# The FFN's down projection: seven-product 2x2 blocks in two sweeps, or the plain product into eight PSUM banks

## The chip, the cores and the metric

The kernel runs on one core of one Trainium2 chip. The metric is the device time of one execution in microseconds (us). The core has TensorE (PE, matrix products; PEld is its loading of the stationary operand), VectorE (DVE), ScalarE (ACT), GpSimd (POOL) and SyncE (SP, which issues most of the DMA transfers). The engines run side by side and wait for one another by semaphores.

## The reference, cut to what matters

One layer of a decoder trunk with 512 tokens, 1024 channels and a feed-forward network (FFN) of 2816 inner channels, all in float32. The change concerns the last product, `@ w_down`, of shape 512x2816 by 2816x1024.

```python
def conv_glu_ffn(h, w_up, conv_w, w_down):
    a, g = jnp.split(h @ w_up, 2, axis=-1)
    return (jax.nn.silu(causal_dwconv(a, conv_w)) * g) @ w_down
...
        h = rmsnorm(x, norm_ffn[l]) * (1 + sc2) + sh2
        x = x + g2 * conv_glu_ffn(h, ffn_w_up[l], ffn_conv_w[l], ffn_w_down[l])
    return rmsnorm(x, final_norm)
```

## The kernel before, in words

**Products in two parts.** Every float32 operand of a large product is split into a rounded part (`hi`, type float32r, a copy by ACT) and the rest (`lo`, a subtraction by DVE). A product is then three matmuls into one PSUM bank: hi by hi, hi by lo, lo by hi. A matmul here takes a stationary operand of 128x128 and a moving one of 128x512 or 128x256.

**Order.** The code names buffers and operations; a scheduler puts the instructions of each engine in one fixed order, by their dependences and by priorities (`tc.high_priority`, `urgent`). An engine works its list off in that order; an instruction that waits holds up all behind it on its engine. SP's list of transfers works the same way.

**Stages.** The branches of the mixer, their gates and the merge come first, then the output projection with the residual, then the FFN's up projection, then its down projection with the closing norm. In the trace the up projection runs from about 820 us on and the down projection from about 1071 us to the end.

**Up projection (lines 1001 to 1203).** For each block `m` of 128 inner channels it forms 2x2 block products, seven in place of eight, in `product` (matmuls of 128x256 at lines 1053 to 1055). DVE's adds at lines 1185, 1194, 1195 and 1201 take the products out of PSUM; the conv is at lines 689 to 691, the gate at line 1202, and the result goes into the tile `f`, 22 blocks of 128x512. Per block, lines 1016, 1017 and 1046 split the weights, and POOL's lines 1034 to 1037 form their sums. The last product of all is `last()` (line 1203), twelve matmuls named `sd<-mg_hi,h_hi` and the like; its bank is free for it once line 1195 has read it. Tile names in a row are those of the memory's first user: `mg_hi`, `mg_lo`, `h_hi` and `h_lo` hold parts of `f` in the down stage.

**Down projection (lines 1205 to 1389).** The 22 blocks of `f` are taken in 11 pairs. The even and odd block of a pair, the two token halves and the two column halves make 2x2 blocks. `sweep1` forms four of the seven products for all pairs, `sweep2` the other three on top of copies of those. Per pair, `sweep1` has

- three sums of `f` blocks on POOL and one on DVE (lines 1266 to 1271), and their splits, line 1249 on ACT and line 1250 on DVE,
- two sums of weight blocks on POOL and one on DVE (lines 1273 to 1275), and the splits of the four weight blocks, line 1236 on ACT and line 1237 on DVE,
- 4 products x 2 token blocks x 3 matmuls of 128x512 (line 1257).

`sweep2` reads the weights again (lines 1242 to 1246), forms sums at lines 1310 to 1312, splits in the same way and has 3 x 2 x 3 matmuls per pair. After the last three pairs, `finish` and `residual` (lines 1333 and 986) multiply by `g2`, add the residual `x_end`, take the norm and store the rows, a token block after another.

**Buffers.** Raw weights land in four buffers (`wraw`), in `sweep2` in `h_hi` and `h_lo` as well. Split weights lie in two rings of three pairs, `whi`/`wlo` and `shi`/`slo`. Split `f` lies in six slots, two in the tiles `h_hi`/`h_lo` and four in `mg_hi`/`mg_lo`; those four are in use by the up projection until `last()` is done.

```python
    def down(ps, i, a, ai, w, wi, first=False, last=False):
        t = slice(i * 128, (i + 1) * 128)
        ops = [(0, 0), (0, 1), (1, 0)]
        for n, (x, y) in enumerate(ops):
            PE.matmul(ps, a[x][:, ai, t], w[y][:, wi], start=first and n == 0, stop=last and n == 2, skip_group_check=True)
```

Of the kernel before, what the change touches and what calls it, by code (L numbers as in the profile page):

```python
# [59 lines left out]
def hybrid_block(ctx, tc, ins, out, consts, dbg=None, stop=99):  # L60
# [196 lines left out]
    def ada_first(c0, n):  # L257
        """Chunks c0..c0+n of the first two parts of the modulation, not yet summed over partitions."""
# [88 lines left out]
    def rel_pos(name, shape, aps, pos0, pool, keep=None):  # L347
        """Positions less the first one, in float32: exact however large they are, as long as the differences are exact."""
# [11 lines left out]
    def bias_operands():  # L360
# [16 lines left out]
        # scaled by a power of two to magnitudes under 2^15, and split into two parts of 11 bits  # L377
# [905 lines left out]
    for j in range(n_pairs):  # L1283
        sweep1(j)
# [136 lines left out]
```

## Time and profile before

| what | value |
|---|---|
| time, median of 3 runs (lowest, highest) | 1248.59 us (1246.18, 1259.89) |
| span of the profiled execution, first to last instruction | 1246.3 us |
| time around that span | none is listed; the median lies 2.3 us above it |
| busy share of the span: PE, DVE, POOL, ACT | 86%, 76%, 42%, 40% |
| mean granted clock of PE | 0.950 |

The page of the profile is of one execution. A busy share is a mean over stages of different kinds; the stretch of a stage, its waits and the order of its instructions say what bounds it. The clock is a fraction of full speed: 1.00 is 2.4 GHz, 0.5 is 1.2 GHz, and a value between is a mixture over time.

### The profile page before, as it was taken

Reading aid. Unit: us, or ns where it says so; the run is one execution under the profiler, and the core shown is the slowest. Engines: PE = TensorE matmul, PEld = TensorE weight load, DVE = VectorE, ACT = ScalarE, POOL = GpSimd, SP = SyncE. Lnnn points to the kernel's source line nnn. Section 1 sums busy time; section 2 is a strip of 40 time slices with the busy share of each in tenths; the row PEclk is TensorE's granted clock in tenths of the full one; section 3 lists DMA queues with packets and bytes.
Section 4 is the critical chain, followed back from the end, with each engine's and each line's share of the span. In section 5 each row is a group of like instructions: output and inputs, shape, how many; then the busy total and the mean of one; then the engine's idle time right before and its main releaser. Section 6 shows DMA issues by size and latency. Waiting matters only on the chain.

```text
span 1246.3 us, 18485 instructions
## 1 busy us (share of the span) xinstructions
PE 1076.5 (86%) x6896; PEld 871.0 (70%) x6896; DVE 945.3 (76%) x1538; ACT 495.6 (40%) x890; POOL 522.9 (42%) x372
## 2 busy tenths in 40 slices
PE   4798999799999799888989999989888887679665
PEld 3676678577667768665666788889888886557444
DVE  6778777532789378976655444899898898999997
ACT  4243422242434244223434333665445454444442
POOL 3232223322222415554541000156566565776762
PEclk9789999899989899988999999989999999899898
DMA  9632123412348933698653535312323232244611
GB/s 313 174 86 71 39 60 102 95 35 66 107 150 253 303 96 86 193 235 218 179 134 98 145 101 166 115 51 85 92 79 101 73 99 85 76 170 168 218 53 68
DMA packets 194247, 156.97 MB, mean 126 GB/s; under 512 B 18499, under 2 KB 167389, under 8 KB 194157
## 3 DMA queue, kind: packets, MB, share of 16 engines
q1 hardware_dynamic: 165773, 131.22, 36.1%
q10 hardware_dynamic: 23056, 14.53, 3.9%
q0 software_dynamic: 5328, 10.03, 3.6%
q8 instruction: 54, 0.88, 0.3%
q14 instruction: 36, 0.29, 0.1%
HBM read 137.13 MB, written 18.63 MB: 125 GB/s over the span
## 4 chain that ended last, share of the span: by engine, by line
PE 39%; DVE 37%; issue 10%; DMA 6%; ACT 4%; POOL 2%; SPq 0%; ACTq 0%; DVEq 0%; POOLq 0%
PE mm L177 6%; PE mm L179 6%; PE mm L178 6%; DVE wlo L1237 3%; DMA xraw<-in_ada_w 3%; DVE acc L217 2%; DVE mg_lo L1250 2%; DVE h_lo L1046 2%; DVE slo L1237 2%; DVE slo L1017 2%; DVE acc L271 2%; PE sd L801 2%; DVE sub L571 1%; PE sd L727 1%; PE sd L800 1%
## 5 line engine op out<-in xcount | busy, mean ns | idle before, releaser
L165 POOL TENSOR_TENSOR wlo<-wraw,whi 128x1024 fp32r<-128x1024 f32 (+1 forms) x70 | 154.2, 2204 | 279.8 <-ACT whi L163 225.7
L178 PE MATMUL mm<-h_lo,whi 128*128 128x512 f32 (+2 forms) x496 | 201.8, 407 | 1.2 <-DVE h_lo L1082 1.2
L177 PE MATMUL mm<-h_hi,whi 128*128 128x512 f32 (+2 forms) x496 | 202.1, 408 | 0.7 <-DVE o_cv L702 0.7
L179 PE MATMUL mm<-h_hi,wlo 128*128 128x512 f32 (+2 forms) x496 | 201.3, 406 | 0.0
L163 ACT ACTIVATE whi<-wraw 128x1024 fp32r<-128x1024 f32 (+1 forms) x86 | 80.1, 934 | 222.2 <-PE mm L178 91.8
L178 PEld LDWEIGHTS mm<-h_lo,whi 128*128 128x128 f32 (+1 forms) x496 | 95.7, 193 | 23.5 <-issue 2.5
L177 PEld LDWEIGHTS mm<-h_hi,whi 128*128 128x128 f32 (+1 forms) x496 | 95.4, 193 | 22.4 <-issue 3.2
L179 PEld LDWEIGHTS mm<-h_hi,wlo 128*128 128x128 f32 (+1 forms) x496 | 95.6, 193 | 21.4 <-issue 1.5
L1053 PE MATMUL sd<-mg_hi,shi 128*128 128x256 f32 x240 | 70.1, 292 | 18.0 <-DVE p L1185 17.8
L1034 POOL TENSOR_TENSOR fS<-wraw 128x512 f32<-128x512 f32 x20 | 29.8, 1490 | 129.2 <-DMA wraw<-in_ffn_w_up 125.6
L217 DVE SCALAR_TENSOR_TENSOR acc<-xraw,ccol,acc 128x512 f32<-128x512 f32 x56 | 60.5, 1080 | 23.0 <-DMA xraw<-in_ada_w 22.5
L1055 PE MATMUL sd<-mg_hi,slo 128*128 128x256 f32 x240 | 68.1, 284 | 0.0
L1054 PE MATMUL sd<-mg_lo,shi 128*128 128x256 f32 x240 | 68.0, 283 | 0.0
L1017 DVE TENSOR_TENSOR slo<-fS,shi 128x1024 fp32r<-128x1024 f32 x40 | 60.5, 1512 | 0.5 <-ACT shi L1016 0.4
L1053 PEld LDWEIGHTS sd<-mg_hi,shi 128*128 128x128 f32 x240 | 45.9, 191 | 21.1 <-DVE p L1185 21.1
L1017 DVE TENSOR_TENSOR wlo<-wraw,whi 128x1024 fp32r<-128x1024 f32 x27 | 34.0, 1260 | 20.2 <-ACT whi L1016 20.1
L1053 PE MATMUL mm<-h_hi,whi 128*128 128x256 f32 x160 | 46.1, 288 | 3.0 <-ACT p L1066 3.0
L721 DVE TENSOR_SCALAR mk<-posq,thr 128x512 f16<-128x512 f32 (+3 forms) x128 | 44.7, 421 | 4.1 <-PE sd L727 4.1
L1016 ACT ACTIVATE shi<-fS 128x1024 fp32r<-128x1024 f32 x40 | 42.1, 1052 | 10.7 <-PE sd L1054 10.5
L1054 PEld LDWEIGHTS sd<-mg_lo,shi 128*128 128x128 f32 x240 | 46.0, 192 | 0.0
L1055 PEld LDWEIGHTS sd<-mg_hi,slo 128*128 128x128 f32 x240 | 45.9, 191 | 0.0
L1054 PE MATMUL mm<-h_lo,whi 128*128 128x256 f32 x160 | 45.6, 285 | 0.0
(565 smaller groups left out, 3120.6 us busy)
## 6 DMA issues: line engine op xcount, KB each, us to landing
wraw<-in_w_in SPq DMA_DIRECT2D x61, 512.0 KB, 4.1
xraw<-in_ada_w SPq DMA_DIRECT2D x96, 256.0 KB, 4.2
wraw<-in_ffn_w_up SPq DMA_DIRECT2D x44, 512.0 KB, 3.8
wraw<-in_ffn_w_down SPq DMA_DIRECT2D x17, 512.0 KB, 3.5
wraw<-in_w_branch SPq DMA_DIRECT2D x24, 256.0 KB, 3.6
bias_d<-stage ACTq DMA_DIRECT2D x10, 512.0 KB, 5.8
wraw<-in_w_o SPq DMA_DIRECT2D x8, 512.0 KB, 3.8
h_hi<-in_ffn_w_down SPq DMA_DIRECT2D x8, 512.0 KB, 4.5
```

Source lines behind the costliest of these rows:

```text
L163: ACT.activation(hi, raw, AF.Copy)
L165: lo_engine[0].tensor_tensor(lo, raw, hi, op=ALU.subtract)
L177: PE.matmul(ps, hi[:, k, :], ahi[:, k0 + k, :], start=start and k == 0, stop=False)
L178: PE.matmul(ps, hi[:, k, :], alo[:, k0 + k, :], start=False, stop=False)
L179: PE.matmul(ps, lo[:, k, :], ahi[:, k0 + k, :], start=False, stop=stop and k == kt - 1)
L217: DVE.scalar_tensor_tensor(acc, raw, ck, acc, op0=ALU.mult, op1=ALU.add)
L721: DVE.tensor_scalar(m_[:, :n], posq[:, b * 128:], thr[:, b, gg:gg + 1], None, op0=ALU.is_ge)
L1017: DVE.tensor_tensor(lo, src, hi, op=ALU.subtract)
L1053: PE.matmul(ps, at(w[0], k), b[0][:, k], start=first and k == 0, stop=False, skip_group_check=True)
L1054: PE.matmul(ps, at(w[0], k), b[1][:, k], start=False, stop=False, skip_group_check=True)
L1055: PE.matmul(ps, at(w[1], k), b[0][:, k], start=False, stop=k == 3, skip_group_check=True)
L1237: DVE.tensor_tensor(lo[:, d], src, hi[:, d], op=ALU.subtract)
```

## The change

The down projection is formed directly. Each of the 22 blocks of `ffn_w_down` (128x1024) is loaded once and split once, by `pair` (line 1016 on ACT, line 1017 on DVE); each pair of `f` blocks is split once, as 128x1024 (line 1219 on ACT, line 1220 on DVE). All eight PSUM banks, four token blocks by two column halves, are filled at once: 22 x 8 x 3 matmuls of 128x512 (lines 1238 to 1240). The sums of blocks, the second reading of the weights and the copies between the sweeps are gone. The last two pairs are kept back and run bank by bank, so that the closing norm of a token block can run while the next is multiplied. The up projection's code is the same. Comments and docstrings are gone from the file too. The core of the diff:

```diff
-    sd, mm = [sd_bank() for _ in range(5)], [mm_bank() for _ in range(3)]
-    p1b, p5b, p6b, p7b = sd[:2], [sd[2], mm[0]], mm[1:], sd[3:]
+    n_pairs, n_tail = 11, 2
+    banks = [mm_bank() for _ in range(3)] + [sd_bank() for _ in range(5)]
...
-    def sweep1(j):
-        ra, rb = rows_of(2 * j, 0, D), rows_of(2 * j + 1, 512, 512)
-        b11, b12 = ra[:, 0:512], ra[:, 512:D]
-        a11, a21, a12, a22 = (f[:, 2 * j + x, t] for x, t in ((0, t1), (0, t2), (1, t1), (1, t2)))
-        u = next_slot()
-        s1, s2, s3 = sn("p1"), sn("p5"), sn("p6")
-        t12 = T("fS", [128, 2, 512], bufs=2, pool=fs.pool)
-        POOL.tensor_tensor(s1, a21, a22, op=ALU.add)
-        DVE.tensor_tensor(s3, a11, a21, op=ALU.subtract)
-        POOL.tensor_tensor(s2, s1, a11, op=ALU.subtract)
-        for i, src in enumerate((a11, s1, s2, s3)):
-            split_a(u, i, src.unsqueeze(1))
-        POOL.tensor_tensor(a21, a12, s2, op=ALU.subtract)
-        with tc.high_priority(offset=4000):
-            POOL.tensor_tensor(t12[:, 0], b12, b11, op=ALU.subtract)
-            POOL.tensor_tensor(t12[:, 1], rb, t12[:, 0], op=ALU.subtract)
-            DVE.tensor_tensor(rb, rb, b12, op=ALU.subtract)
-        w12 = w_tile(2, (b11, t12[:, 0]))
-        w34 = w_tile(2, (t12[:, 1], rb))
...
-    def sweep2(j):
...
-        split_a(u, 0, ff_flat[:, j * 1024 + N2:(j + 1) * 1024].rearrange("p (i t) -> p i t", t=N2))
-        t4 = T("fS", [128, 2, 512], bufs=2, pool=fs.pool)
-        with tc.high_priority(offset=4000):
-            DVE.tensor_tensor(t4[:, 0], rb[:, 0:512], rb[:, 512:D], op=ALU.subtract)
-            POOL.tensor_tensor(t4[:, 1], ra[:, 512:D], ra[:, 0:512], op=ALU.subtract)
-            POOL.tensor_tensor(t4[:, 0], t4[:, 0], t4[:, 1], op=ALU.add)
-        w56 = w_tile(2, (rb,))
-        w7 = w_tile(1, (t4[:, 0],))
...
+    def split_pair(j):
+
+        u = slots[j if j < 2 else 2 + (j - 2) % 4]
+        src = ff_flat[:, j * 1024:(j + 1) * 1024].rearrange("p (a t) -> p a t", t=u[0].shape[2])
+        ACT.activation(u[0], src, AF.Copy)
+        DVE.tensor_tensor(u[1], src, u[0], op=ALU.subtract)
+        return u
...
+    def w_down(m):
+        raw = load_raw([128, D], [((lambda r: r), dram("ffn_w_down", m * 128 * D, [[D, 128], [1, D]]))])
+        ring = n_ring[0] // 3 % 2
+        n_ring[0] += 1
+        return pair([128, D], raw, ws if ring else None)
+
+    def down(tb, hf, u, m, w, first=False, last=False):
+        ps, c = banks[tb * 2 + hf], slice(hf * 512, hf * 512 + 512)
+        hi, lo = (f_cols(x, m, tb) for x in u)
+        PE.matmul(ps, hi, w[0][:, c], start=first, stop=False)
+        PE.matmul(ps, hi, w[1][:, c], start=False, stop=False)
+        PE.matmul(ps, lo, w[0][:, c], start=False, stop=last)
...
     for j in range(n_pairs):
-        s = sweep2(j)
...
+        u = split_pair(j)
+        for m in range(2):
+            w = w_down(2 * j + m)
+            if j >= n_pairs - n_tail:
+                tail.append((u, m, w))
+                continue
+            for tb in range(4):
+                for hf in range(2):
+                    down(tb, hf, u, m, w, first=j == 0 and m == 0)
+        if j == 1:
             SP.dma_start(g2, g2_d)
...
+        if 2 <= j < 6:
+            SP.dma_start(x_end[j - 2], x1_d[j - 2])
+        if j == 6:
+            SP.dma_start(fnorm, dram("final_norm", 0, [[0, 128], [1, D]]))
             ACT.activation(sqrt_table, one, AF.Sqrt)
...
+    for tb in range(4):
+        for hf in (1, 0):
+            for t_ in tail:
+                down(tb, hf, *t_, last=t_ is tail[-1])
+            residual(x_end[tb], hf, banks[tb * 2 + hf], g2, ss[:, tb])
+            if hf:
+                POOL.tensor_tensor(x_end[tb][:, c_hi], x_end[tb][:, c_hi], fnorm[:, c_hi], op=ALU.mult)
+        finish(tb)
```

The instructions of every engine stand in the same order in both programs up to the last blocks of the up projection. The first place is DVE there, between the read of block 20's bank (the first `L1195` row; `p` with a number is a block's copied product) and the read of block 21's bank (the second), behind which `last()` starts. Before, in `L1237`, `L1275` the down stage's work:

```order
L1195 TENSOR_TENSOR wk<-sd,p_9905 128x256
L1237 TENSOR_TENSOR wlo<-wraw,whi 128x512 x2
L1237 TENSOR_TENSOR slo<-fS,shi 128x512
L1275 TENSOR_TENSOR wraw<-wraw 128x512
L1237 TENSOR_TENSOR wlo<-fS,whi 128x512
L1202 TENSOR_TENSOR f<-f,wk 128x512
L1185 TENSOR_TENSOR p_9986<-sd,p_9810 128x256
L1237 TENSOR_TENSOR slo<-wraw,shi 128x512 x2
L1194 TENSOR_TENSOR wk<-sd,p_9986 128x256
L1275 TENSOR_TENSOR wraw<-wraw 128x512
L1237 TENSOR_TENSOR slo<-fS,shi 128x512
L1195 TENSOR_TENSOR wk<-sd,p_9985 128x256
```

The same place in the changed program, where the splits of whole weight blocks (`slo<-wraw`) are the down stage's work:

```order
L1195 TENSOR_TENSOR wk<-sd,p_9905 128x256
L1201 TENSOR_TENSOR wk<-sd,p_9552 128x256
L1017 TENSOR_TENSOR slo<-wraw,shi 128x1024
L1202 TENSOR_TENSOR f<-f,wk 128x512
L690 SCALAR_TENSOR_TENSOR f<-wk,fw,f 128x511
L1201 TENSOR_TENSOR wk<-sd,p_9681 128x256
L691 SCALAR_TENSOR_TENSOR f<-wk,fw,f 128x510
L1185 TENSOR_TENSOR p_9986<-sd,p_9810 128x256
L1017 TENSOR_TENSOR slo<-wraw,shi 128x1024
L1194 TENSOR_TENSOR wk<-sd,p_9986 128x256
L1202 TENSOR_TENSOR f<-f,wk 128x512
L1195 TENSOR_TENSOR wk<-sd,p_9985 128x256
```

Nine operations of the down stage have become two of twice the width, and five of the up stage's own (line 1201 twice, lines 690, 691 and 1202, of earlier blocks) have moved in.

The second place is DVE within the down stage: `mg_lo` rows split `f`, `wlo` and `slo` rows split weights, `fS` rows form sums of weights. Before, early in the second sweep:

```order
L1250 TENSOR_TENSOR mg_lo<-f,mg_hi 128x768
L1237 TENSOR_TENSOR slo<-h_hi,shi 128x1024
L1250 TENSOR_TENSOR mg_lo<-f,mg_hi 128x768
L1237 TENSOR_TENSOR slo<-fS,shi 128x512
L1310 TENSOR_TENSOR fS<-h_lo 128x512
L1237 TENSOR_TENSOR wlo<-h_hi,whi 128x1024
L1250 TENSOR_TENSOR mg_lo<-f,mg_hi 128x768
L1237 TENSOR_TENSOR wlo<-fS,whi 128x512
```

In the changed program, from behind `last()` on:

```order
L1220 TENSOR_TENSOR mg_lo<-f,mg_hi 128x1024 x4
L1017 TENSOR_TENSOR wlo<-wraw,whi 128x1024 x3
L1017 TENSOR_TENSOR slo<-wraw,shi 128x1024 x2
L1220 TENSOR_TENSOR mg_lo<-f,mg_hi 128x1024
L1017 TENSOR_TENSOR slo<-wraw,shi 128x1024
L1017 TENSOR_TENSOR wlo<-wraw,whi 128x1024
L1220 TENSOR_TENSOR mg_lo<-f,mg_hi 128x1024
```

All sums are gone from the list; from here on it holds 16 weight blocks and 9 pairs of `f`, and then the closing norm.

The third place is SP's list of transfers, which shows where loads other than weights stand. `f<-g_d` is the row `g2`, `f<-x_d` the residual rows; both land in parts of `f` and wait until those have been split. Before, around the turn from the first to the second sweep, where the weights come in blocks and half blocks and into `h_hi` too:

```order
L147 DMA wraw<-in_ffn_w_down 128x1024
L147 DMA wraw<-in_ffn_w_down 128x512
L147 DMA wraw<-in_ffn_w_down 128x1024
L1245 DMA h_hi<-in_ffn_w_down 128x1024
L147 DMA wraw<-in_ffn_w_down 128x512
L147 DMA wraw<-in_ffn_w_down 128x1024
```

In the changed program, the whole stage:

```order
L147 DMA wraw<-in_ffn_w_down 128x1024 x2
L1269 DMA f<-g_d 128x1024
L147 DMA wraw<-in_ffn_w_down 128x1024 x3
L1271 DMA f<-x_d 128x1024
L147 DMA wraw<-in_ffn_w_down 128x1024 x5
L1271 DMA f<-x_d 128x1024 x3
L147 DMA wraw<-in_ffn_w_down 128x1024
L1273 DMA f<-in_final_norm 128x1024
L147 DMA wraw<-in_ffn_w_down 128x1024 x11
L1255 DMA out_dram<-f 128x512 x8
```

Each block of the weights now appears once, 22 in all, and the other loads stand among the first eleven.

## Rows read from the trace of the kernel before

**Rows 1.** The page, part 1: busy time, share of the span, instructions.

```profile
PE 1076.5 (86%) x6896; PEld 871.0 (70%) x6896; DVE 945.3 (76%) x1538; ACT 495.6 (40%) x890; POOL 522.9 (42%) x372
```

**Rows 2.** Windows: stretch, length, busy per engine, PE's clock, DMA share, GB/s.

```profile
680.00:780.00 100.00, 100.00 (x447) 80.16 (x446) 46.45 (x62) 38.83 (x57) 7.67 (x8) 1.00 0.50 140
1028.95:1072.59 43.64, 30.70 (x231) 28.99 (x230) 38.45 (x46) 19.55 (x36) 28.82 (x22) 0.96 0.27 86
1072.59:1235.60 163.01, 122.82 (x470) 91.84 (x468) 159.18 (x185) 67.00 (x128) 104.71 (x75) 0.92 0.36 127
```

**Rows 3.** Waits of PE from 1072.5 to 1236 us: total, times, longest.

```profile
PE sd L1257 <- DVE mg_lo L1250: 18.3, 8, 4.9
PE sd L1257 <- DVE slo L1237: 9.5, 3, 7.2
PE mm L1257 <- DVE h_lo L1250: 4.7, 1, 4.7
PE sd L1257 <- DVE wlo L1237: 3.8, 4, 1.4
PE sd L1257 <- ACT f L1292: 2.1, 2, 1.5
PE mm L1257 <- DVE mg_lo L1250: 1.8, 2, 1.2
```

**Rows 4.** Timeline of PE, places in the down stage: start, duration, instruction.

```profile
1073.83 0.28 PE L1055 MATMUL sd<-mg_hi,h_lo 128*128 128x256 f32 x1
...
1120.13 0.63 PE L1257 MATMUL sd<-shi,mg_hi 128*128 128x512 f32 x1
1120.56 0.63 PE L1257 MATMUL sd<-slo,mg_hi 128*128 128x512 f32 x1
...
1227.02 0.39 PE L1257 MATMUL sd<-whi,mg_hi 128*128 128x512 f32 x1
...
1235.19 0.39 PE L1257 MATMUL sd<-whi,mg_lo 128*128 128x512 f32 x1
```

**Rows 5.** Timeline of DVE, end of the up projection; in brackets its wait.

```profile
1035.74 0.41 DVE L1195 TENSOR_TENSOR wk<-sd,p 128x256 f32<-128x256 f32 x1
...
1037.21 0.95 DVE L1250 TENSOR_TENSOR h_lo<-f,h_hi 128x256 fp32r<-128x256 f32 x1
1039.35 0.69 DVE L1237 TENSOR_TENSOR wlo<-wraw,whi 128x512 fp32r<-128x512 f32 x1 [1.18 <-ACT whi L1236]
...
1053.82 1.20 DVE L1275 TENSOR_TENSOR wraw<-wraw 128x512 f32<-128x512 f32 x1 [2.19 <-POOL fS L1274]
...
1071.24 0.68 DVE L1237 TENSOR_TENSOR slo<-fS,shi 128x512 fp32r<-128x512 f32 x1
1071.84 0.41 DVE L1195 TENSOR_TENSOR wk<-sd,p 128x256 f32<-128x256 f32 x1
```

**Rows 6.** Groups of instructions by shape, 880 us on: busy us, mean ns.

```profile
L1017 DVE TENSOR_TENSOR wlo<-wraw,whi 128x1024 fp32r<-128x1024 f32 x12 | 14.6, 1213 | 3.9 <-ACT whi L1016 3.9
L1016 ACT ACTIVATE whi<-wraw 128x1024 fp32r<-128x1024 f32 x12 | 12.7, 1061 | 15.5 <-DMA wraw<-in_ffn_w_up 15.5
...
L1250 DVE TENSOR_TENSOR mg_lo<-f,mg_hi 128x768 fp32r<-128x768 f32 x11 | 16.8, 1536 | 0.0
```

**Rows 7.** The page, part 6: transfers, KB each, median us to landing.

```profile
wraw<-in_ffn_w_down SPq DMA_DIRECT2D x17, 512.0 KB, 3.5
```

**Rows 8.** Timeline of DVE and ACT in the last ten microseconds.

```profile
1236.67 0.68 DVE L1336 TENSOR_TENSOR wk<-sd,f 128x512 f32<-128x512 f32 x1
1236.77 0.63 ACT L993 ACTIVATE wk<-f 128x512 f32<-128x512 f32 x1 [1.17 <-DVE ss L232]
1237.30 0.18 ACT L993 ACTIVATION_READ_ACCUMULATOR wk<-f 128x1 f32 x1
1237.59 1.78 DVE L1337 TENSOR_TENSOR f<-f,wk 128x512 f32<-128x512 f32 x1
1240.69 0.15 DVE L1342 SCALAR_TENSOR_TENSOR ss<-ss 128x1 f32<-128x1 f32 x1
```

More of the change, by code (lines that the diff above doesn't have):

```diff
@@ L1239, in w_tile @@
-        return hi, lo
-    def rows_of(m, c0, n, dst=None):
-        src = dram("ffn_w_down", m * 128 * D + c0, [[D, 128], [1, n]])
-        if dst is None:
-            return load_raw([128, n], [((lambda r: r), src)])
-        SP.dma_start(dst, src)
-        return dst
-    def split_a(u, i, src):
-        ACT.activation(u[0][:, i:i + src.shape[1]], src, AF.Copy)
-        DVE.tensor_tensor(u[1][:, i:i + src.shape[1]], src, u[0][:, i:i + src.shape[1]], op=ALU.subtract)
-    def down(ps, i, a, ai, w, wi, first=False, last=False):
-        t = slice(i * 128, (i + 1) * 128)
-        ops = [(0, 0), (0, 1), (1, 0)]
-        for n, (x, y) in enumerate(ops):
-            PE.matmul(ps, a[x][:, ai, t], w[y][:, wi], start=first and n == 0, stop=last and n == 2, skip_group_check=True)
@@ L1283, in hybrid_block @@
-    for j in range(n_pairs):
-        sweep1(j)
-    piece = lambda j: f[:, j:j + 4:2, t1]
-    as2 = lambda v: v.rearrange("p (i t) -> p i t", i=2)
-    p1, p7, p5 = [piece(14), piece(18)], [piece(6), piece(10)], [wk(), wk()]
-    with urgent():
-        for b, dst in ((p1b, p1), (p5b, [as2(x) for x in p5]), (p7b, p7)):
-            for i in range(2):
-                ACT.activation(dst[i], as2(b[i]), AF.Copy)
-        for i in range(2):
-            DVE.tensor_tensor(p1[i], p1[i], as2(p6b[i]), op=ALU.add)
+        return pair([128, D], raw, ws if ring else None)
@@ L1333, in finish @@
-    def finish(tb, bank, add):
-        x, t, v = x_end[tb], wk(), ss[:, tb, 0:1]
-        with urgent():
-            DVE.tensor_tensor(t, bank, g2[:, c_lo], op=ALU.mult)
-            add.tensor_tensor(x[:, c_lo], x[:, c_lo], t, op=ALU.add)
-            if add is DVE:
-                DVE.tensor_tensor_reduce(t, x[:, c_lo], x[:, c_lo], 1.0, 0.0, op0=ALU.mult, op1=ALU.add, accum_out=v)
-            else:
-                ACT.activation(t, x[:, c_lo], AF.Square, accum_out=v)
-            DVE.scalar_tensor_tensor(v, v, 1.0 / D, ss[:, tb, 1:2], op0=ALU.mult, op1=ALU.add)
-            rstd = rsqrt_of(v, 1)
+    g2, x_end, fnorm = late(0), [late(1 + tb) for tb in range(4)], late(5)
@@ L1350, in hybrid_block @@
     for j in range(n_pairs):
-        s = sweep2(j)
-        if j >= n_pairs - n_tail:
-            tail.append(s)
-        else:
-            for b in (p1b, p5b, p7b):
-                for i in range(2):
-                    down(b[i], i, *s[id(b)])
-        if j == 0:
-            SP.dma_start(g2, g2_d)
-        if j in (1, 2):
-            SP.dma_start(x_end[j + 1], x1_d[j + 1])
-        if j in (3, 4):
-            i = j - 3
-            POOL.tensor_tensor(p7[i], p7[i], as2(p5[i]), op=ALU.add)
-            POOL.tensor_tensor(p7[i], p7[i], p1[i], op=ALU.add)
-            add_g2(2 + i, 0, p1[i])
-            add_g2(2 + i, 1, p7[i])
-            t = wk()
-            ACT.activation(t, x_end[2 + i][:, 512:], AF.Square, accum_out=ss[:, 2 + i, 1:2])
@@ L1370, in hybrid_block @@
-        if j in (5, 6):
-            tb = j - 5
-            SP.dma_start(x_end[tb], x1_d[tb])
-            add_g2(tb, 1, p1[tb])
-        if j == 7:
-            ACT.activation(sqrt_table, one, AF.Sqrt)
-            SP.dma_start(fnorm, dram("final_norm", 0, [[0, 128], [1, D]]))
-            high_half(2)
-            high_half(3)
-    def rest(bank, i):
-        for s in tail:
-            down(bank[i], i, *s[id(bank)], last=s is tail[-1])
-        return bank[i]
-    for i in range(2):
-        finish(2 + i, rest(p7b, i), POOL)
@@ L1386, in hybrid_block @@
-    for i in range(2):
-        residual(x_end[i], 1, rest(p5b, i), g2, ss[:, i])
-        high_half(i)
-        finish(i, rest(p1b, i), DVE)
+        u = split_pair(j)
[8 more added lines that the diff above has]
+        if j == 1:
+            SP.dma_start(g2, g2_d)
```

52 lines of the change are left out of this document (10 added, 42 removed).

## The prediction

> **What bounds the kernel now.** The page's first part [rows 1] shows PE busy for 86% of the span and VectorE for 76%, which by itself points at PE. It is a mean over stages, so the next view is the windows, cut at the stage that changes [rows 2]. In the down stage, from 1072.59 us on, VectorE is busy for 159.18 of 163.01 us and GpSimd for 104.71; PE has 122.82 us of modelled busy time and a mean granted clock of 0.92. The reader should see that VectorE has no free time there while PE has. The view of waits says the same from the other side [rows 3]: PE waits 40.2 us in this stretch (the sum of the six rows), all but 2.1 of it for splits (`lo` parts of weights and of `f`) that VectorE makes.
>
> The timeline of PE gives the rate that it could have [rows 4]. The last 35 steps before the last matmul, 1227.02 to 1235.19 us, are 8.17 us: 0.2334 us from one 128x512 matmul to the next, with nothing to wait for. The old stage has 11 x (4 + 3) x 2 x 3 = 462 matmuls. Five start before the up projection's last matmul at 1073.83 us; the others take until 1235.19 us, 161.4 us. At 0.2334 us, 457 of them are 106.7 us. The difference, 54.7 us, is 40.2 us of waits and 14.5 us of matmuls that ran slower than that: after waits the rows show 0.43 us from start to start (1120.13 to 1120.56 us), the rate of the lower of the two clock levels, 1.2 GHz. So the stage is bound by VectorE, and PE pays twice: it waits, and its clock falls after it has waited.
>
> **The change part by part.** *PE's work.* 22 x 8 x 3 = 528 matmuls of the same shape in place of 462: 66 more, 66 x 0.2334 = 15.4 us. Four of them stand ahead of the up projection's last product in PE's list, 524 behind it. Their steps at the full rate are 523 x 0.2334 = 122.1 us. That 0.2334 us holds over such a length rests on the stretch from 680 to 780 us, in which PE was busy for 100.00 of 100 us at a granted clock of 1.00 [rows 2]; its 447 recorded matmuls would make it 0.2237 us, which I keep as the short end (117.0 us).
>
> The Trainium skill, page "TensorE: Matmul & The Clock Gate", section "Back-to-back issue gap", gives N / 2.4 + 2.5 ns between matmuls at full clock, which is 215.7 ns for 512 columns. The trace disagrees: 233.4 ns in 35 steps in a row. By the page the 523 steps would be an estimated 112.8 us in place of 122.1; by the trace they are 122.1, and the trace decides.
>
> *VectorE's work.* All sums of blocks go (per pair five on POOL and two on VectorE in the first sweep, two and one in the second), as do the second splits of weights. What is left behind `last()` is 16 weight blocks and 9 pairs of `f`, all 128x1024. The short price is 1.213 us [rows 6]. The long one comes from the 128x768 splits in the old stage, 1.536 us while POOL is at work beside them: 2.05 us for 1024 columns. That is 25 x 1.213 = 30 us to 25 x 2.05 = 51 us, in 122 us of PE work. POOL has four operations left in the whole stage, so I take the short price; VectorE is free for more than half of the stage either way, and the 54.7 us of waits and slow matmuls go. ACT's splits (1.061 us each) stay beside this.
>
> *What is late next: the loads.* A weight block needs 3.5 us from issue to landing [rows 7], 1.061 us on ACT and 1.213 us on VectorE, 5.8 us. PE works on it for 24 x 0.2334 = 5.6 us. One block at a time this would just fail to keep up, but four raw buffers and six split pairs stand ahead of PE, so up to ten blocks are under way. SP's list also holds `g2`, four residual rows and the norm's row; each waits for a pair of `f` to be split, and the weights queued behind it wait too. These splits stand first behind `last()` in VectorE's list and need no weights, and PE then has six split blocks, 33 us of work. I cost the loads at nothing; if that cover fails, it is the first rival below.
>
> *The end of the up projection.* Here VectorE's list decides when `last()` may start. From the read of block 18's bank to that of block 21's, 1035.74 to 1071.84 us, 36.1 us go by [rows 5]. In them stand 16 operations of the down stage, the first at 1037.21 and the last at 1071.24 us; with the waits before them (1.18 and 2.19 us are the longest) they take 19.8 us, which leaves 16.3 us of the up projection's own. The changed list has seven in their place, five blocks of weights and two pairs of `f`: 7 x 1.213 = 8.5 us (14.4 at 2.05). Four more operations of the up projection come earlier, one of 0.41 us and three of 512 columns. Those lie between 0.68 and 1.78 us [rows 8]; at 1.0 us the four are 3.4 us (2.5 to 5.7). New is a wait for the first weight blocks: the first landed so late that ACT's copy kept VectorE waiting to 1039.35 us, and a whole block's copy is longer and has less to hide it. I take 4 us for two such waits (0 to 5). Queued behind them are the adds that release PE's next products, so they count in full. Sum: 16.3 + 8.5 + 3.4 + 4 = 32.2 us, so the read comes at 1067.9 us in place of 1071.84. PE's last product then ended 2.0 us after it, and dense matmuls start at about 1070 us. The bounds are 27.3 us (1065) and 41.4 us (1079, five later than before).
>
> *The tail.* After the last matmul's end (1235.19 + 0.39 = 1235.58 us) the old kernel needs 10.7 us to 1246.3. In the new one VectorE is not behind: 0.68 us for the product with `g2`, 0.68 for the sum, 0.81 on ACT for the squares, then as from 1240.69 us on, which is 5.6 us to the end [rows 8], and some 0.4 us for one more small operation and the steps between engines: 8.2 us. The bounds are 8.0 and, as before, 10.7.
>
> **The sum** for the profiled execution: 1070 + 122.1 + 0.4 + 8.2 = 1200.7 us against 1246.3, 45.6 us less. Told by parts: 54.7 us of waits and slow matmuls go, 15.4 us of matmuls come, the up projection ends some 4 us earlier and the tail is 2.5 us shorter. The median of the runs lies 2.3 us above the span, so I forecast **1203 us**.
>
> **The rivals.** *Loads become the bound.* If the buffers did not run ahead, every block behind the first six would take the chain at its long price, 3.5 + 1.06 + 2.05 = 6.6 us against 5.6: 16 us more, 1219 us. For it speaks that SP's list mixes loads that wait for splits with the weights. Against it: the ten blocks ahead, and a mean of 127 GB/s in the old stage [rows 2], which moves more bytes than the new one needs. Chance 0.07.
>
> *PE falls to the lower clock and stays there: slower than before.* The clock fell in the old stage behind PE's waits. If the new stage kept enough small waits, at 0.43 us a step it would last 224.9 us, and the kernel 1306 us. It decides from a mean step of (1246.3 - 8.2 - 0.4 - 1070) / 523 = 0.321 us, that is from 44% of the matmuls at the lower level. Against it: 100 us of unbroken work at 1.00, and no split that PE must wait for after the first. Chance 0.03.
>
> *The matmuls follow one another faster than in any row.* With no engine writing to the memory as often as in the old stage, a step could shrink to 512 columns at 2.4 GHz and little more, 215.7 ns, and the time would be 1194 us. That is the page's rule above. Against it, the 35 steps were at 0.2334 us while VectorE was not hindering PE. Chance 0.04.
>
> *It does not do what it says.* VectorE stays the bound and the waits come back under other names, within 1% of before. It would have to be busy for some 160 us with work that I price at 30 to 51 us and the norm. Chance 0.03.
>
> **How the numbers follow.** My forecast has 0.83. Its own ends are the sums of the bounds: 1065 + 117.0 + 0.4 + 8.0 = 1190 us and 1079 + 122.1 + 0.4 + 10.7 + 2.3 = 1214.5 us, with some 2.5 us for two spells at the lower clock 1217. All low ends together are less likely than the high ones, so the range is 1192 to 1217 us, and takes in the faster matmuls; it leaves out the loads, the slow clock and no change, and the outermost of my own case, together under 0.2. One per cent is about what a measurement of this kernel can tell from no change. Faster by over 1%: 0.83 + 0.07 + 0.04 = 0.94; within 1%: 0.03; slower: 0.03.
>
> **What would show it.** In the new profile: 528 matmuls at lines 1238 to 1240, most 0.233 us apart, at a granted clock near 1.00; waits of PE in the stage of a few us in all; VectorE busy for less than half of it, POOL nearly idle; the up projection's last product between 1063 and 1077 us; 8 to 11 us from the last matmul to the end. I am wrong if PE still waits for `lo` parts or for weights by tens of us, or if its clock stays below 0.9 in the dense stretch.

## The result, and the profile after

| | before | after |
|---|---|---|
| median of 4 runs each, us (lowest, highest) | 1249.78 (1246.18, 1259.89) | 1206.03 (1200.61, 1215.32) |
| ratio, 95% interval | | 0.9643 (0.958 to 0.9706) |
| span and own time of the profiled execution, us | 1246.3, not listed | 1198.9, 1200.61 |
| last matmul of the up projection to the last of all, starts, us | 161.36 | 122.14 |

The changed kernel is faster by 3.6%; 1203 us was forecast. An execution that is some per cent slower as a whole, at a lower granted clock than others of the same kernel, is left out where kernels are compared; the profiled one of the eighth experiment was such, so its stretch is read from the tenth's profile, which has the same up projection.

The page's first part, beside [rows 1]:

```profile
PE 1074.5 (90%) x6962; PEld 876.1 (73%) x6962; DVE 824.0 (69%) x1405; ACT 463.2 (39%) x800; POOL 412.6 (34%) x289
```

VectorE lost 121.3 us of busy time and GpSimd 110.3, while PE has 66 matmuls more and is busy for about as long as before. The windows, beside [rows 2] (stretch, length, busy time of PE, PEld, DVE, ACT and POOL, PE's clock, DMA share, GB/s); the third is the stretch by which the experiments are compared:

```profile
1028.95:1066.00 37.05, 30.95 (x238) 29.77 (x237) 33.49 (x41) 19.32 (x28) 13.44 (x10) 0.95 0.50 161
1066.00:1191.00 125.00, 123.34 (x534) 98.98 (x532) 48.74 (x67) 35.23 (x48) 5.66 (x4) 1.00 0.25 85
1066.81:1188.95 122.14, 122.14 (x527) 98.17 (x525) 45.95 (x64) 34.04 (x45) 4.38 (x3) 1.00 0.24 83
```

In the second row VectorE is busy for 39% of the stage in place of 98%, PE for 99%, and the granted clock is 1.00 in place of 0.92. The waits of PE from 1040 us to the end, beside [rows 3], are two, both ahead of the stage:

```profile
PE sd L1053 <- DVE wk L1195: 3.1, 1, 3.1
PE sd L1053 <- DVE p L1185: 1.3, 1, 1.3
```

The timeline of PE, beside [rows 4] (start, duration, instruction):

```profile
1066.81 0.28 PE L1055 MATMUL sd<-mg_hi,h_lo 128*128 128x256 f32 x1
1066.93 0.39 PE L1239 MATMUL mm<-wlo,h_hi 128*128 128x512 f32 x1
...
1188.95 0.39 PE L1240 MATMUL sd<-shi,mg_lo 128*128 128x512 f32 x1
```

From the second row to the last are 523 steps in 122.02 us, 0.2333 us each. The old stage had this rate only in spells between its waits, one of them the 44 steps up to its last matmul (1224.92 to 1235.19 us). The timeline of VectorE at the up projection's end, beside [rows 5]:

```profile
1036.19 0.41 DVE L1195 TENSOR_TENSOR wk<-sd,p 128x256 f32<-128x256 f32 x1
...
1040.27 1.76 DVE L1017 TENSOR_TENSOR wlo<-wraw,whi 128x1024 fp32r<-128x1024 f32 x1 [2.54 <-ACT whi L1016]
...
1047.41 2.29 DVE L1017 TENSOR_TENSOR wlo<-wraw,whi 128x1024 fp32r<-128x1024 f32 x1
...
1064.98 0.41 DVE L1195 TENSOR_TENSOR wk<-sd,p 128x256 f32<-128x256 f32 x1
```

The read of block 21's bank (the last row) comes 28.8 us behind that of block 18 (the first), where it was 36.1. The splits of the stage by shape, beside [rows 6], at the short price, and the weights' transfers on the page's part 6, beside [rows 7], whose median is unchanged:

```profile
L1017 DVE TENSOR_TENSOR wlo<-wraw,whi 128x1024 fp32r<-128x1024 f32 x9 | 11.0, 1223 | 22.0 <-ACT whi L1016 22.0
L1220 DVE TENSOR_TENSOR mg_lo<-f,mg_hi 128x1024 fp32r<-128x1024 f32 x9 | 10.8, 1222 | 20.7 <-ACT mg_hi L1219 20.7
```

```profile
wraw<-in_ffn_w_down SPq DMA_DIRECT2D x22, 512.0 KB, 3.5
```

VectorE now waits for ACT's copies, which wait for buffers that PE has yet to read. The tail, beside [rows 8]:

```profile
1189.44 1.28 POOL L1281 TENSOR_TENSOR f<-f 128x512 f32<-128x512 f32 x1 [4.39 <-ACT wk L993]
1189.51 0.68 DVE L991 TENSOR_TENSOR wk<-sd,f 128x512 f32<-128x512 f32 x1
1190.23 1.04 DVE L992 TENSOR_TENSOR f<-f,wk 128x512 f32<-128x512 f32 x1
...
1193.51 0.75 DVE L1253 SCALAR_TENSOR_TENSOR f<-f,ss 128x512 f32<-128x512 f32 x1
```

From the last matmul's end, 1188.95 + 0.39 = 1189.34 us, to the end of the span are 9.56 us.

### The profile page after: what moved, and what is told of

It reads as the page before. It is cut to its first block, busy times and chain, and to the rows that moved or that the text cites. A ratio compares the mean times of both kernels' runs of the same rounds, so it can differ in the third digit from the quotient of the medians.

```text
span 1198.9 us, 18180 instructions
## 1 busy us (share of the span) xinstructions
PE 1074.5 (90%) x6962; PEld 876.1 (73%) x6962; DVE 824.0 (69%) x1405; ACT 463.2 (39%) x800; POOL 412.6 (34%) x289
## 5 line engine op out<-in xcount | busy, mean ns | idle before, releaser
L165 POOL TENSOR_TENSOR wlo<-wraw,whi 128x1024 fp32r<-128x1024 f32 (+1 forms) x70 | 158.0, 2259 | 269.8 <-ACT whi L163 221.3
L1017 DVE TENSOR_TENSOR wlo<-wraw,whi 128x1024 fp32r<-128x1024 f32 x39 | 50.8, 1302 | 42.2 <-ACT whi L1016 42.2
L1016 ACT ACTIVATE whi<-wraw 128x1024 fp32r<-128x1024 f32 x39 | 41.3, 1058 | 64.8 <-PE sd L1240 24.8
L1281 POOL TENSOR_TENSOR f<-f 128x512 f32<-128x512 f32 x4 | 5.7, 1416 | 124.6 <-ACT wk L993 124.6
```

Of the source, the lines that this page charges most:

```text
L165: lo_engine[0].tensor_tensor(lo, raw, hi, op=ALU.subtract)
L1016: ACT.activation(hi, src, AF.Copy)
L1017: DVE.tensor_tensor(lo, src, hi, op=ALU.subtract)
```

## The experiments

Theory A is the prediction's: VectorE's work held the old stage, and the new one is as long as its matmuls, 0.2333 us each. Rivals B to E are that VectorE still sets the pace (B), that VectorE's busy time was a symptom of GpSimd's sums or of the loads (C), that GpSimd's traffic held up the matmuls themselves (D), and that the loads set the pace (E). What the first eight runs showed raised theory G against H, on why VectorE had so much to do. Experiments with a single run are read by their stretch (from the start of the up projection's last matmul to that of the last of all), since the same code ahead of the up projection differs by up to 22 us from one execution to the next (its first matmul at line 1055 stands between 818.3 and 840.8 us).

### 1 and 2. More work for VectorE in the changed kernel

```diff
+        if m >= 6:
+            with tc.high_priority(offset=4000):
+                for _ in range(3):
+                    DVE.tensor_tensor(junk, raw[:, 0:512], raw[:, 512:D], op=ALU.subtract)
```

> Adds three subtractions of 128x512 on VectorE, into a scratch tile that nobody reads, to each of the 16 weight blocks from the seventh on: 48 operations at the 0.68 us that such a shape takes undisturbed, about 33 us of VectorE time. Theory A (VectorE bound the old stage, the matmuls at 0.2333 us each bound the new one): VectorE was busy for 48.7 of 125 us, so the 33 us fit in; the dense stretch stays at 122.0 us within 2 us, PE waits for nothing in it, and the time stays within 1% of the changed kernel's. Rival B (VectorE still sets the pace under other names): the stretch grows by about 33 us, to 155.

Measured: 1202.97 us. The window of the stretch:

```profile
1068.49:1190.64 122.15, 122.15 (x526) 98.26 (x525) 75.97 (x111) 34.58 (x46) 4.37 (x3) 1.00 0.25 82
```

Thirty microseconds more of VectorE (45.95 to 75.97) moved nothing: the stretch is 122.15 us (122.14 without them) and the clock 1.00. B falls. The second has `range(12)`:

> The same with twelve subtractions in each of the 16 blocks: 192 operations of 0.61 to 0.68 us, 117 to 131 us on top of the 48.7 us that VectorE has now. Theory A: VectorE becomes the bound again, with some 166 to 180 us of work in the stage; the stretch from the up projection's last matmul to the last matmul of all grows from 122 to about 165 to 180 us (the added operations begin with the seventh block, part of them before the stretch), PE waits for lo parts of weights by 25 to 50 us, and its granted clock falls below 1.00 behind the waits. That would be the old stage made anew without its blocks. Rival C (the old stage was held by GpSimd's sums or by its loads, VectorE's busy time was a symptom of those): PE keeps its rate, and the stretch stays under 130 us, or grows by the bare excess over 122 us with the clock at 1.00.

Measured: 1254.11 us, span 1251.7. The stretch and what follows it, and PE's waits in the stage:

```profile
1069.85:1210.01 140.16, 127.93 (x526) 100.68 (x525) 135.82 (x186) 27.89 (x30) 0.00 (x0) 0.96 0.20 64
1210.01:1251.70 41.69, 0.40 (x2) 0.00 (x0) 39.70 (x79) 9.17 (x23) 5.43 (x4) 0.55 0.13 51
```

```profile
PE mm L1243 <- ACT whi L1016: 9.2, 3, 3.9
PE mm L1243 <- ACT shi L1016: 2.3, 2, 1.4
PE mm L1244 <- DVE wlo L1017: 0.7, 1, 0.7
```

The direction is A's, its numbers for the stretch are not: 140.2 us in place of 165 to 180, and 12.2 us of waits in place of 25 to 50. The blocks split ahead kept PE from waiting until 1164 us (its first wait of the stage, 1.37 us, ends at 1165.73), and 39 of the scratch operations came behind the last matmul. Over both rows VectorE was busy for 175.5 of 181.9 us, so it is the bound again. PE's waits stand under ACT's name, and ACT waited 17.6 us in all for the scratch operations. The clock is 0.96 and PE waits, which C does not have; what held the old stage is left to experiments 6, 7 and 9. The end comes 1251.7 - 1198.9 = 52.8 us later, 3.0 of it from a later start; 132.6 us of scratch less the 76.2 us that VectorE had free would be 56.4.

### 3. GpSimd at work beside the new stage

```diff
+        if m >= 6:
+            with tc.high_priority(offset=4000):
+                for _ in range(4):
+                    POOL.tensor_tensor(junk, raw[:, 0:512], raw[:, 512:D], op=ALU.subtract)
```

> Adds four subtractions of 128x512 on GpSimd, into a scratch tile, to each of the 16 weight blocks from the seventh on: 64 operations of about 1.0 to 1.3 us, 65 to 85 us beside the matmuls, as much as GpSimd's sums were in the old stage or a little less. Theory A: VectorE's splits beside them go from 1.22 us to between 1.5 and 2.3 us, VectorE's busy time from 48.7 to 55 to 70 of 125 us, and the stretch stays at 122 us within 2 us, with the granted clock at 1.00. Rival D (what the change gave back was the traffic of GpSimd and VectorE together, which held up the matmuls themselves): the matmuls come more than 0.24 us apart, and the stretch grows by 5 us or more.

Measured: 1200.43 us. The window of the stretch, and groups of VectorE and of GpSimd in the stage (busy us, mean ns):

```profile
1066.54:1188.98 122.44, 122.41 (x527) 98.11 (x525) 68.77 (x64) 33.92 (x45) 103.90 (x62) 1.00 0.24 82
```

```profile
L1017 DVE TENSOR_TENSOR wlo<-wraw,whi 128x1024 fp32r<-128x1024 f32 x9 | 18.9, 2120 | 6.9 <-ACT whi L1016 6.9
L1221 DVE TENSOR_TENSOR mg_lo<-f,mg_hi 128x1024 fp32r<-128x1024 f32 x9 | 18.0, 2024 | 18.9 <-ACT mg_hi L1220 18.9
```

```profile
L1237 POOL TENSOR_TENSOR junk<-wraw 128x512 f32<-128x512 f32 x59 | 100.1, 1696 | 4.6
```

As A has it. With GpSimd as busy as in the old stage (103.9 us) VectorE's splits rose from 1.22 to about 2.0 us, and the matmuls kept their rate. D falls for the new stage: GpSimd does not hinder PE here (122.44 us against 122.14). That it costs VectorE so much made experiment 7 worth a run.

### 4. Every weight block loaded twice

```diff
-        raw = load_raw([128, D], [((lambda r: r), dram("ffn_w_down", m * 128 * D, [[D, 128], [1, D]]))])
+        raw = load_raw([128, D], [((lambda r: r), dram("ffn_w_down", m * 128 * D, [[D, 128], [1, D]]))] * 2)
```

> Loads each of the 22 blocks of w_down twice into its buffer, so that the stage moves 23 MB in place of 11.5 MB. Theory A: the loads have room (the core's DMA engines were busy for 0.25 of the stage at 85 GB/s; twice that is 0.5 and 170 GB/s), the stretch stays at 122 us within 2 us; the first weight blocks come 1 to 3 us later, which may move the stretch's start by as much. Rival E (the loads are next in line: 3.5 us for a block by itself, 7 us for two in turn, 7 + 1.06 + 1.22 = 9.3 us of chain against 5.6 us of matmuls): if the buffers do not run ahead, PE waits for hi and lo parts, and the stretch grows by 16 us or more, up to 22 x 3.7 = 81 us.

Measured: 1211.86 us, which is the execution's late start: its first matmul of the up projection at line 1055 stands at 836.5 us against 825.5. The window of the stretch:

```profile
1079.72:1201.17 121.45, 121.45 (x523) 97.71 (x522) 45.87 (x64) 33.92 (x45) 4.39 (x3) 1.00 0.44 154
```

The stretch is no longer (121.45 us against 122.14) with 154 GB/s in place of 83. E falls, with a factor of nearly two in hand.

### 5. As many matmuls as the old stage had

```diff
+        n_mm[0] += 1
+        if n_mm[0] % 8 not in (2, 5, 7):
-        PE.matmul(ps, hi, w[1][:, c], start=False, stop=False)
+            PE.matmul(ps, hi, w[1][:, c], start=False, stop=False)
```

> Leaves out the product hi x lo in three of every eight of the stage's 176 groups, 66 of 528 matmuls, so that 462 are left, as many as in the old stage; the output lacks these terms. Theory A: PE is the bound at 0.2333 us per matmul, so the stretch shrinks by 66 x 0.2333 = 15.4 us, from 122.0 to 106.6 us, and the time with it. Rival E (something beside PE, loads or splits, is only just hidden): the stretch shrinks by less than 10 us and PE gets waits, since a block then lasts 21 x 0.2333 = 4.9 us on PE against 5.8 us of load, copy and split in turn.

Measured: 1203.02 us in an execution whose up projection began 15.3 us late (840.8 against 825.5 us). The window of the stretch:

```profile
1083.73:1190.46 106.73, 106.73 (x460) 85.80 (x459) 45.49 (x60) 33.47 (x44) 4.35 (x3) 1.00 0.27 91
```

122.14 - 106.73 = 15.41 us for 66 matmuls, as A has it: the new stage is as long as its matmuls, and the 15.4 us that the change adds are real.

### 6. The kernel before without VectorE's splits

```diff
-                DVE.tensor_tensor(lo[:, d], src, hi[:, d], op=ALU.subtract)
-        return hi, lo
+        return hi, hi
...
-        DVE.tensor_tensor(u[1][:, i:i + src.shape[1]], src, u[0][:, i:i + src.shape[1]], op=ALU.subtract)
```

> The kernel before, with its two sweeps, its sums of blocks and its 462 matmuls, but without VectorE's splits in the down stage (the lo parts of weights and of f are not made, and the matmuls that read them read the hi parts in their place, so the output lacks the small parts). GpSimd's sums, the loads and ACT's copies stay. Theory A: with VectorE's load down from 159 to some 50 us, PE's waits for it (38 of 40.2 us) go and the clock comes back to near 1.00; the stage from the up projection's last matmul to the last of the stage falls from 161.4 to 107 to 120 us, the span to 1190 to 1208 us. Rival D or E (GpSimd's sums or the loads of the two sweeps set the pace): the stage stays above 145 us, and the waits turn up under POOL's or the queue's name.

Measured: 1192.54 us, span 1190.8. From the up projection's last matmul at 1071.44 us to the start of the last group of three matmuls, which is 0.47 us before that of the last:

```profile
1071.44:1179.33 107.89, 107.58 (x458) 86.15 (x457) 49.09 (x61) 65.24 (x122) 83.02 (x68) 0.99 0.55 187
```

The old stage falls from 161.4 to 108.4 us with its sums, its two sweeps and its second reading of the weights in place (187 GB/s, GpSimd busy for 83 us). VectorE's splits held it, and D and E are out for the old stage too.

### 7. The kernel before without GpSimd's sums

```diff
-        POOL.tensor_tensor(s1, a21, a22, op=ALU.add)
-        POOL.tensor_tensor(s2, s1, a11, op=ALU.subtract)
-        POOL.tensor_tensor(a21, a12, s2, op=ALU.subtract)
-            POOL.tensor_tensor(t12[:, 0], b12, b11, op=ALU.subtract)
-            POOL.tensor_tensor(t12[:, 1], rb, t12[:, 0], op=ALU.subtract)
...
-            POOL.tensor_tensor(t4[:, 1], ra[:, 512:D], ra[:, 0:512], op=ALU.subtract)
-            POOL.tensor_tensor(t4[:, 0], t4[:, 0], t4[:, 1], op=ALU.add)
```

> The kernel before, with the sums that GpSimd makes in the down stage left out (the splits read unsummed blocks of weights and of f in their place, so the output is another); every split of VectorE and all 462 matmuls stay. It tells how much of VectorE's 159 us was the number of its operations and how much was GpSimd at work beside them. Theory A in its plain form (the number of operations): a 128x512 split stays near 1.0 us and the stage shrinks by less than 15 us of 161.4. Rival D' (the slowing beside GpSimd was the larger part): the splits fall to 0.68 us (1.2 us for 1024 columns), VectorE's busy time to some 105 us, and the stage to 115 to 130 us, without one matmul or split less.

Measured: 1191.69 us, span 1190.0. The window of the stretch, and two groups of splits in it:

```profile
1065.58:1178.89 113.31, 110.11 (x461) 87.12 (x459) 102.46 (x177) 66.52 (x125) 20.90 (x9) 0.97 0.53 183
```

```profile
L1250 DVE TENSOR_TENSOR mg_lo<-f,mg_hi 128x768 fp32r<-128x768 f32 x11 | 12.5, 1146 | 0.0
L1237 DVE TENSOR_TENSOR wlo<-wraw,whi 128x512 fp32r<-128x512 f32 x16 | 10.3, 683 | 0.1
```

The plain form of A falls, and D' holds, a little under its 115 to 130 us. With every split and every matmul in place the stage is 113.3 us, and VectorE's time is 102.5 us. The same 11 splits of 768 columns took 1536 ns before [rows 6] and take 1146 ns now. What the sums cost was VectorE's time, though another engine made them. That much is left of C: GpSimd's sums made 48.1 us of the old stage (161.4 less 113.3), by way of VectorE.

### 9. GpSimd's sums made on VectorE

This run follows from the last one. All seven sums of a pair that stand in the diff above go to the busy engine, and nothing is left out:

```diff
-        POOL.tensor_tensor(s1, a21, a22, op=ALU.add)
+        DVE.tensor_tensor(s1, a21, a22, op=ALU.add)
...
-            POOL.tensor_tensor(t4[:, 0], t4[:, 0], t4[:, 1], op=ALU.add)
+            DVE.tensor_tensor(t4[:, 0], t4[:, 0], t4[:, 1], op=ALU.add)
```

> The kernel before with the seven sums that GpSimd makes for each pair in the down stage made on VectorE instead; nothing is left out, and VectorE, the busy engine, gets 77 operations more. Theory G (VectorE's time in the old stage was swollen by GpSimd at work beside it): without the sums VectorE was busy for 97.8 of 108.6 us. The sums on VectorE at its undisturbed prices are 11 x (3 x 0.416 + 2 x 0.68) = 28.7 us in the first sweep and 11 x 2 x 0.68 = 15.0 us in the second, 141 us in all, less than the 159 us that it had with GpSimd's help. The stage falls from 161 to 140 to 152 us, and the median from about 1253 to some 1235 to 1243 us. Theory H (the number of VectorE's operations is what counts; GpSimd took work off it): 159 + 44 = 203 us of VectorE, and the kernel becomes some 40 us slower.

Measured in 4 runs: median 1234.28 us (1230.56 to 1243.33), just under the range expected; ratio to the kernel before 0.9834 (0.9757 to 0.9911). The window of the stretch, a group of splits, and the largest of PE's waits:

```profile
1072.76:1215.57 142.81, 118.80 (x445) 89.35 (x445) 132.49 (x232) 66.79 (x124) 20.16 (x9) 0.91 0.40 135
```

```profile
L1250 DVE TENSOR_TENSOR mg_lo<-f,mg_hi 128x768 fp32r<-128x768 f32 x11 | 12.5, 1147 | 0.0
```

```profile
PE sd L1257 <- DVE mg_lo L1250: 13.4, 8, 3.5
```

G holds and H falls by the sign: the bound engine got 77 operations more, and the kernel became 1.7% faster. The size is less sure than the sign: the mean of these four is 1235.6 us, that of the four executions of the kernel before that are compared with them 1250.3 us (1241.91 to 1256.09), which is 1.2%. In that stretch VectorE is busy for 132.5 us with GpSimd's sums among its work, against 159.18 us without them in [rows 2].

### 11. Three kinds of work on GpSimd

```diff
+                if m < 14:
+                    POOL.tensor_scalar(junk[:, 0:1], raw[:, 0:1], 1.0, None, op0=ALU.mult)
+                for _ in range(8 if m < 14 else 4):
+                    if m < 14:
+                        POOL.memset(junk, 0.0)
+                    else:
+                        POOL.tensor_scalar(junk, raw[:, 0:512], 1.0, None, op0=ALU.mult)
```

> The changed kernel with scratch work on GpSimd beside the splits, of two kinds: for weight blocks 6 to 13 one tiny operation of one column that waits for the block and then eight memsets of 128x512, which read nothing; for blocks 14 to 21 four copies of 128x512 with one input. Two-input subtractions there made VectorE's 128x1024 splits 2.02 us in place of 1.22. Theory G1 (what stretches a split is GpSimd reading at the same time): splits beside the memsets stay at 1.22 us, beside the copies they are longer, 1.5 us or more. Theory G2 (any work on GpSimd stretches them): both do. Theory G3 (only two-input operations): neither. The time of the whole stays within 1% of the changed kernel's under all three.

Measured: 1197.81 us. Groups of VectorE, first from 1060 to 1098.6 us (beside memsets), then from 1098.7 to 1151.7 us (beside 32 copies with one input):

```profile
L1221 DVE TENSOR_TENSOR mg_lo<-f,mg_hi 128x1024 fp32r<-128x1024 f32 x5 | 5.8, 1219 | 4.1 <-ACT mg_hi L1220 4.1
L1017 DVE TENSOR_TENSOR slo<-wraw,shi 128x1024 fp32r<-128x1024 f32 x4 | 4.9, 1220 | 8.8 <-ACT shi L1016 8.8
...
L1017 DVE TENSOR_TENSOR wlo<-wraw,whi 128x1024 fp32r<-128x1024 f32 x6 | 9.5, 1578 | 12.2 <-ACT whi L1016 12.2
L1017 DVE TENSOR_TENSOR slo<-wraw,shi 128x1024 fp32r<-128x1024 f32 x4 | 6.5, 1638 | 3.1 <-ACT shi L1016 3.1
L1221 DVE TENSOR_TENSOR mg_lo<-f,mg_hi 128x1024 fp32r<-128x1024 f32 x5 | 6.1, 1226 | 19.4 <-ACT mg_hi L1220 19.4
```

G1 holds in the main: beside memsets, which read nothing, a split stays at 1.22 us; beside one-input copies the two groups of weights take 1.58 and 1.64 us in the mean. In the timeline nine of these ten stand at 1.63 to 1.66 us and one at 1.23, as do the five of `f`. What tells them apart is where in a copy a split begins. Two copies on GpSimd, each with the split that began behind it:

```profile
1119.79 1.49 POOL L1242 TENSOR_SCALAR junk<-wraw 128x512 f32<-128x512 f32 x1
1120.46 1.23 DVE L1221 TENSOR_TENSOR mg_lo<-f,mg_hi 128x1024 fp32r<-128x1024 f32 x1 [3.70 <-ACT mg_hi L1220]
...
1126.26 1.49 POOL L1242 TENSOR_SCALAR junk<-wraw 128x512 f32<-128x512 f32 x1
1126.29 1.66 DVE L1017 TENSOR_TENSOR slo<-wraw,shi 128x1024 fp32r<-128x1024 f32 x1 [3.06 <-ACT shi L1016]
```

The split that began 0.67 us into a copy was not held up; the one that began 0.03 us into one was, by 0.4 us. Of the six short splits, four began 0.67 to 1.14 us into a copy; the other two began ahead of one, and then the copy was held up instead (1.92 and 2.56 us in place of 1.49). Of the nine long ones, four began 0.02 to 0.03 us into a copy, and five into a copy that the split before had itself held up (1.67 to 2.14 us).

### 8 and 10. Both projections direct

The up projection has sums on GpSimd and splits on VectorE of the same kind, so it was formed directly as well. The blocks from the third on become

```diff
+        wa, wg = pair([128, 8, 128], up_raw(m * 128)), pair([128, 8, 128], up_raw(DFF + m * 128), ws)
+        pa, pg = mm_bank(), sd_bank()
+        mm_t(pa, wa, h2)
+        mm_t(pg, wg, h2)
+        t = wk()
+        conv3(t, pa, fw[:, m, :])
+        ACT.activation(t, t, AF.Silu)
+        DVE.tensor_tensor(f[:, m, :], t, pg, op=ALU.mult)
```

> The changed kernel with the up projection done directly as well: its 20 row blocks of seven products become two direct products of 24 matmuls each, 128x512, so that the whole FFN has no 2x2 blocks any more; the sums on GpSimd and VectorE go, and two splits of 1024 columns are left for each block in place of four and a half. Theory A says that sums and splits, not matmuls, are the dear part there too: a block lasts 12.2 us now with VectorE busy for nearly all of it; direct it has 48 x 0.2333 = 11.2 us of matmuls and some 5 us of VectorE. Expected: 20 blocks x 1.0 us, about 20 us less than the changed kernel, a median near 1186 us (1175 to 1195), with the granted clock at 1.00 to the end. Rival F (in the up projection the blocks pay, since PE is the bound there at 84 half-wide matmuls per block): the time is the changed kernel's or up to 20 us longer.

Measured in 4 runs: median 1184.95 us, ratio to the kernel before 0.9438 (0.9369 to 0.9507), below the changed kernel's interval. The tenth adds one edit in the tail:

```diff
-                POOL.tensor_tensor(x_end[tb][:, c_hi], x_end[tb][:, c_hi], fnorm[:, c_hi], op=ALU.mult)
+                DVE.tensor_tensor(x_end[tb][:, c_hi], x_end[tb][:, c_hi], fnorm[:, c_hi], op=ALU.mult)
```

> The kernel with both projections direct, and the four products of the tail's high half with the norm's row on VectorE in place of GpSimd, so that nothing of GpSimd runs beside VectorE's last sums. From the last matmul's end to the end of the span went 9.6 us; the last sum beside GpSimd's product took 1.04 us and should take 0.68, so 0.4 us less, about 9.2. That is below what the runs can tell as a time; the median should lie where the version with both projections direct lay, 1176 to 1191 us. Rival: the product on VectorE delays the last residual, and the tail is 0.3 us longer.

Measured in 4 runs: median 1178.62 us, ratio 0.9369 (0.9307 to 0.9431). The window from the last transpose of `h` to the up projection's last matmul, first of the changed kernel, then of this one:

```profile
813.10:1066.81 253.71, 220.80 (x1775) 213.56 (x1774) 232.27 (x257) 131.31 (x213) 147.38 (x104) 0.99 0.32 96
```

```profile
805.50:1039.84 234.34, 234.34 (x1050) 190.49 (x1050) 104.94 (x117) 80.70 (x100) 0.00 (x0) 1.00 0.35 106
```

The up projection loses 19.4 us, as A expected (20); F falls. VectorE goes from 92% of that window to 45%, and PE is busy in all of it. The tail of this version:

```profile
1164.72 0.69 DVE L992 TENSOR_TENSOR f<-f,wk 128x512 f32<-128x512 f32 x1
```

With GpSimd out of the way the last sum takes 0.69 in place of 1.04 us, and 9.03 us go by from the last matmul's end (1162.97 + 0.40) to the end of the span at 1172.4, against 9.56. The two versions' intervals overlap, so as a time this edit can't be told from none. Its median is the lowest of the study, but the eighth's three executions that are compared have a median of 1179.05 us.

## Why the prediction was right, point by point

**The bound of the old stage.** Right, and shown by experiment 6: without VectorE's splits the stage is 108.4 us. How the time came about was only in part foreseen: the prediction counted VectorE's operations and left open how much of their time was their own. Experiments 7 and 9 settle it. With the sums left to GpSimd the stage is 161.4 us, with the sums on VectorE 142.8, with none 113.3. So 18.6 us of the old stage went because making the sums beside the splits is dearer than making them between the splits, and 29.5 us more for the sums themselves. The direct form, without sums, gives 8.8 us of that back in matmuls (122.1 against 113.3).

**54.7 us of waits and slow matmuls go.** Right: no wait of PE is left in the stage, and the clock is 1.00.

**15.4 us of matmuls come.** Right: 0.2333 us a step over 523 steps, 122.0 us against 122.1, and 15.41 us in experiment 5. The short end of 0.2237 us was a misreading: 36 of the 447 matmuls in its stretch have fewer than 512 columns.

**VectorE's remaining work.** The short price was the right choice: 1.22 us. Experiment 3 shows the long one, 2.0 us, to be that of GpSimd's company; at either, VectorE has time to spare, as experiment 1 shows.

**Loads at nothing.** Right, with room: experiment 4.

**The end of the up projection.** 28.8 us where 32.2 were summed. Of the terms, the seven splits took 10.7 us in place of 8.5, since three of them (1.76, 2.29 and 1.75 us) met sums of GpSimd's; the waits for the first weight blocks were one of 2.54 us in place of two of 2; the up projection's own operations, with those moved in, took 28.8 - 10.7 - 2.5 = 15.6 us in place of 19.7, and line 690 stands at 0.73 us where it took 1.75 before. GpSimd was busy for 13.44 of 37.05 us there, against 28.82 of 43.64 in [rows 2]. The dense matmuls start at 1066.9 us, 3.1 us ahead of the 1070.

**The tail.** Under-sized by 1.4 us: 9.56 against 8.2. Its sum took the residual's sum at 0.68 us, but GpSimd's product by the norm's row ran beside it and made it 1.04, which is 0.4 us of the miss. The other 1.0 us lies behind the start of VectorE's last operation (1193.51 us), from which the end of the span is 5.4 us away, where it was 4.4 before (1241.89 to 1246.3 us); what made that last scaling and store longer is open.

**The median.** The profiled execution took 1200.61 us, 2.4 below the forecast. On its span, 1200.7 us was forecast and 1198.9 came: dense matmuls that began 3.1 us early and a tail that was 1.4 us long cancel in part. The median of the four runs lies 7.1 us above that span, since their spans go from 1198.9 to 1213.6 us, where the prediction had taken 2.3. So the median's nearness to the forecast (3.0 us) is in part luck: the span came out short and the distance of the median long.

**The rivals.** The clock did not fall, the loads did not bind, VectorE did not stay the bound. The faster matmuls at 215.7 ns did not come: 233.3 ns held with VectorE idle for three fifths of the time, and in experiment 1 with VectorE busy for as much of it, so what sets that step is not VectorE's writing; what does is open. The Trainium skill, page "TensorE: Matmul & The Clock Gate", section "Back-to-back issue gap", calls the formula that the prediction quotes the gap of a matmul by itself, and gives about 131 ns for a stream of weight loads and matmuls of 512 columns. This stage is such a stream, and its 233.3 ns agree with neither.

## What to carry to other kernels

A seven-product block form saves matmuls and pays in sums; count what the sums cost the engine that splits, at prices read while both engines work. Work given to GpSimd is not taken off VectorE when both read the on-chip memory at the same time: here giving it back to the busy engine was faster, and beside memsets, which read nothing, a split kept its 1.22 us. A busy share near 100% doesn't tell work from being held up, so compare the same shape's mean duration with and without company before deciding what to remove.

## What the runs showed of the hardware that was not expected

A two-input subtraction of 128x1024 on VectorE takes 1.22 us alone, 1.22 beside GpSimd's memsets, 1.63 to 1.66 beside its one-input copies in nine of fifteen cases, and 1.90 to 2.12 in the mean of a group beside its two-input subtractions. GpSimd's own subtraction of 128x512 takes 1.30 us where nothing holds it up, and 1.70 in the mean there. PE's rate and clock don't change beside them (122.44 us).

In experiment 3 the two engines take turns, and the one that began second waits:

```profile
1145.33 1.30 POOL L1237 TENSOR_TENSOR junk<-wraw 128x512 f32<-128x512 f32 x1
1145.47 2.24 DVE L1221 TENSOR_TENSOR mg_lo<-f,mg_hi 128x1024 fp32r<-128x1024 f32 x1 [4.13 <-ACT mg_hi L1220]
```

Splits that began 0.14, 0.53, 0.93 and 1.15 us into a subtraction of 1.3 us took 2.24, 1.84, 1.45 and 1.24 us: each is late by what was left of about 1.15 us. A split that began 0.07 us ahead of one took 1.22 us, and the subtraction 2.31. The Trainium skill, page "SBUF — State Buffer", section "SBUF: two separate sides", has VectorE operations with two inputs from the memory and GpSimd operations that read it take a shared pair of ports in turn, each for a whole instruction, while PE never waits. The rows of the subtractions agree. Those of the copies agree only in part: a copy of 1.49 us held up no split that began 0.67 us into it.
